# One hybrid RWKV-7 and RG-LRU step: the clock by which the scheduler orders the instructions is that of the timeline simulator

## Chip, cores and metric

The kernel runs on 1 core of one Trainium2 chip. The metric is the time of one execution in microseconds (us), the median of several runs. The engines are TensorE (PE in the rows; PEld is its weight load), VectorE (DVE), ScalarE (ACT), GpSimd (POOL) and SyncE (SP, which starts transfers).

## What is computed

One layer over 1152 tokens (128 of context, 1024 latent) of width 1024. An input projection feeds two token mixers side by side: RWKV-7 with 8 heads of 64 in two directions, and a bidirectional RG-LRU of 512 channels. Their outputs go through one output projection, and a gated feed-forward part with a convolution follows (inner width 2816).

```python
h = rmsnorm(x, lp['ln1_g']) * (1.0 + sc1) + sh1
proj = h @ lp['w_in']
r, k, v, xw, xa, xg, xb, gb = jnp.split(proj, SPLITS, axis=-1)
ya, s_fin = rwkv7_mix(r, k, v, xw, xa, xg, s0, ...)
yb, h_fin = rglru_mix(xb, gb, h0, ...)
x = x + g1 * (jnp.concatenate([ya, yb], axis=-1) @ lp['w_out'])
h = rmsnorm(x, lp['ln2_g']) * (1.0 + sc2) + sh2
u = dwconv(h @ lp['w_up'], ...)
ua, ub = jnp.split(u, 2, axis=-1)
x = x + g2 * ((jax.nn.gelu(ua) * ub) @ lp['w_down'])

def _wkv7_step(S, inp):          # per token, in both directions
    sa = jnp.einsum('dbhij,dbhj->dbhi', S, kk_t)
    S = S * w_t[..., None, :] - sa[..., :, None] * b_t[..., None, :] + v_t[..., :, None] * k_t[..., None, :]
    y = jnp.einsum('dbhij,dbhj->dbhi', S, r_t)
```

The bonus of RWKV-7 and the norms of its keys are sums over the 64 channels of a head; the kernel makes them on TensorE as small matmuls whose output has the tokens on the partitions (`cols2`).

## The kernel before

All products are in fp32, split into a high and a low part: one product is three matmuls, and the helper `mm` (L92) records all of them, so that the rows on TensorE have line 92 and are told apart by their tiles. A high part is rounded by L106 or L108, the low part is the remainder (L112).

The kernel is written as generators whose steps alternate at given rates (`beside`, `run_all`). That fixes the order in which the program is written. From it the language's scheduler makes one queue for each engine: it goes through the instructions with a simulated clock, takes among those that the clock says are ready the one written first, and so decides what stands behind what. On the chip each engine then works through its queue in that order and stops at an instruction whose input or buffer is not there. The stages, with the times of the profiled run:

- Start, 0 to 45 us: loads, first norm, transposes.
- A, 45 to 458 us: projections (tile mm; weights winp), one weight tile after the other, each in three spans of 384 tokens. Beside them run, as background generators, the preparation of the scan by `stage_ab`: rates and scaled keys on VectorE (L607 to L640), products dg, the bonus (kd on GpSimd, L669 and L670, then the head sums ab<-rkc,kd on TensorE and the copy bon at L503), the key norms (head sums uk, copy nsq at L503, key k at L572), and for each of four head pairs one `inverse` of 32x32 triangular blocks: a transpose (L510), 30 pairs of L517 and L519 on VectorE, transposes to T (L524) and TT (L526), then two rounds of matmuls iv with a ScalarE copy a2 (L539) between and the copy to TT (L553) behind, which is spilled to DRAM (L707). Values v are copied to vt (ScalarE, L825) and vr (VectorE, L826) and transposed on TensorE (pv, L832).
- B, 458 to 733 us: two scan lanes a and b. A lane goes through its 128-token tiles in hops of 64 tokens: G (mask, L1087, VectorE) from pa<-kxa,BK; Kt from transposes of BK (L1094); y from the state S and from G; R (L1077), V, the state's update (L1185, VectorE); outputs o (L1196, L1198). Beside them runs the rest of the projection with the RG-LRU: convolution taps (L853, VectorE), gates (matmuls lg, L898 on ScalarE), L909 to L919 with sqrt and exp on ScalarE, scans (L929).
- C, 733 to 967 us: four lanes a to d, the head norms of finished tiles (`post`, L1304 to L1322), the modulation vectors (md) and the RG-LRU half of the output projection (wo, gated in at L1408 and L1409).
- D, 967 to 1064 us: the RWKV half of the output projection and the second norm. E and F, from 1064 us on: up-projection (x, y, z, v) and down-projection (acc).

The lanes' buffers reuse the space of the inverse, so the lanes' first loads wait for the last spill of TT. The change touches the last lines of `kernel`; all that is told above lies in `tile_hybrid_step`, which it calls.

## Time and profile before

| | us |
|---|---|
| median of 3 runs (1865.54 to 1865.95) | 1865.56 |
| the profiled execution | 1856.04 |
| its span | 1854.3 |
| TensorE busy | 1699.7 |
| VectorE busy | 1271.6 |
| ScalarE busy | 852.6 |
| GpSimd busy | 727.1 |

The profiled execution is 9.5 us shorter than the median of the runs; 1.7 us of it lie outside the span. The mean granted clock of TensorE is 0.948 of full speed. The rows come from five views: the page; windows, which give the busy time of each engine in a stretch; waits, which sum an engine's idle time by the line that waited and what released it; the timeline, one engine's instructions in order with the idle time before each; and groups, which put alike instructions together.

### The profile page before, as it was taken

To read this page: it belongs to the slowest core of one execution; us is meant where nothing else is said; L and a number is where in the kernel's file an instruction comes from. 1 tells how busy PE (TensorE), PEld (TensorE's weight loads), DVE (VectorE), ACT (ScalarE), POOL (GpSimd) and SP (SyncE) were. 2 spreads that over 40 slices of the span, in tenths; PEclk is the share of its full clock that TensorE was granted. 3 is DMA by queue.
4 is the path that set the end of the run, shared out by engine and by line. 5 is a ranking of instruction groups with operands and counts; after the bars stand their busy time and mean duration, and the time that the engine had idled before them with its cause. 6 is when DMAs were issued, how large, how long until landed. Compare 5 with 4: busy or idle time off the path is not lost.

```text
span 1854.3 us, 35789 instructions
## 1 busy us (share of the span) xinstructions
PE 1699.7 (92%) x13365; PEld 1465.5 (79%) x13365; DVE 1271.6 (69%) x2635; ACT 852.6 (46%) x1763; POOL 727.1 (39%) x742
## 2 busy tenths in 40 slices
PE   5997889788999989799997789999999999999996
PEld 4786868588778778456665689999999999788885
DVE  6458797884467664467788867777777668576764
ACT  6456554642656666334324844444444443121211
POOL 1023332321254354131111076666666664434340
PEclk9998898898989999899998899999999999999998
DMA  8255454443433433856776222222222225548571
GB/s 299 63 163 155 163 162 148 149 128 120 128 107 97 134 103 112 267 192 228 232 245 209 103 65 84 72 72 73 82 73 72 74 81 169 187 161 262 179 247 57
DMA packets 268429, 264.94 MB, mean 143 GB/s; under 512 B 21173, under 2 KB 218448, under 8 KB 268256
## 3 DMA queue, kind: packets, MB, share of 16 engines
q1 hardware_dynamic: 252496, 245.97, 41.7%
q10 hardware_dynamic: 15472, 16.54, 2.6%
q8 instruction: 106, 1.74, 0.4%
q14 instruction: 67, 0.55, 0.1%
q0 software_dynamic: 288, 0.14, 0.0%
HBM read 188.00 MB, written 74.58 MB: 142 GB/s over the span
## 4 chain that ended last, share of the span: by engine, by line
PE 63%; DVE 7%; DMA 3%; issue 3%; ACT 3%; POOL 2%; SPq 0%; DVEq 0%; ACTq 0%; POOLq 0%
PE acc L92 14%; PE x L92 7%; PE y L92 7%; PE z L92 7%; PE mm L92 6%; PE v L92 3%; PE wo L92 3%; PE lg L92 2%; PE ya L92 2%; PE md L92 2%; PE pa L92 2%; PE yb L92 1%; PE ca L92 1%; PE pb L92 1%; PE cb L92 1%
## 5 line engine op out<-in xcount | busy, mean ns | idle before, releaser
L92 PE MATMUL mm<-h_hi,winp 128*128 128x384 f32 x1056 | 307.8, 363 | 6.9 <-DVE vr L826 5.9
L92 PEld LDWEIGHTS mm<-h_hi,winp 128*128 128x128 f32 x1056 | 204.2, 201 | 14.9 <-DVE vr L826 7.0
L92 PE MATMUL mm<-h_lo,winp 128*128 128x384 f32 x528 | 189.6, 360 | 3.7 <-DVE h_lo L112 3.7
L112 POOL TENSOR_TENSOR wl<-raw,wh 128x512 fp32r<-128x512 f32 x110 | 155.3, 1413 | 71.2 <-ACT wh L106 70.8
L106 ACT ACTIVATE wh<-raw 128x512 fp32r<-128x512 f32 x110 | 69.3, 632 | 149.0 <-PE z L92 81.0
L92 PE MATMUL x<-f_hi,wh 128*128 128x256 f32 (+1 forms) x352 | 105.9, 301 | 8.9 <-ACT q L1652 5.3
L92 PEld LDWEIGHTS mm<-h_lo,winp 128*128 128x128 f32 x528 | 106.4, 202 | 6.9 <-DVE h_lo L112 5.0
L1090 POOL TENSOR_TENSOR BK<-BK,pc 128x256 f32<-128x256 f32 x72 | 47.6, 663 | 157.2 <-PE pa L92 59.7
L92 PE MATMUL y<-t_hi,wh 128*128 128x320 f32 (+1 forms) x352 | 104.9, 298 | 0.9 <-DVE q L1657 0.9
L92 PE MATMUL x<-f_lo,wh 128*128 128x256 f32 (+1 forms) x352 | 105.5, 300 | 0.2 <-DVE f_lo L112 0.2
L92 PE MATMUL x<-f_hi,wl 128*128 128x256 f32 (+1 forms) x352 | 105.3, 299 | 0.0
L92 PE MATMUL y<-t_lo,wh 128*128 128x320 f32 (+1 forms) x352 | 104.7, 298 | 0.0
L92 PE MATMUL y<-t_hi,wl 128*128 128x320 f32 (+1 forms) x352 | 104.5, 297 | 0.0
L112 POOL TENSOR_TENSOR wl<-S,wh 128x512 fp32r<-128x512 f32 x44 | 57.5, 1308 | 105.7 <-ACT wh L106 105.7
L92 PE MATMUL acc<-f_hi 128*128 128x512 f32 x330 | 88.9, 390 | 2.7 <-ACT zf L1760 2.7
L108 POOL TENSOR_SCALAR t_hi<-raw 128x512 fp32r<-128x512 f32 x66 | 55.8, 846 | 76.0 <-PE acc L92 33.5
L1619 DVE SCALAR_TENSOR_TENSOR zf<-C,fcw,zf 128x567 f32<-128x567 f32 x66 | 63.0, 955 | 23.4 <-ACT zf L1617 23.4
L92 PEld LDWEIGHTS x<-f_hi,wh 128*128 128x128 f32 x352 | 67.9, 193 | 9.9 <-ACT q L1652 5.8
L92 PEld LDWEIGHTS acc<-f_hi 128*128 128x128 f32 x330 | 61.8, 188 | 15.9 <-ACT zf L1760 3.1
L112 DVE TENSOR_TENSOR t_hi<-raw,t_hi 128x512 fp32r<-128x512 f32 x66 | 47.0, 715 | 35.3 <-POOL t_hi L108 35.3
L1617 ACT ACTIVATE zf<-C,colB,fcw 128x576 f32<-128x576 f32 x66 | 57.2, 867 | 29.9 <-DVE C L1689 15.4
L92 PEld LDWEIGHTS x<-f_lo,wh 128*128 128x128 f32 x352 | 68.0, 193 | 0.5 <-DVE f_lo L112 0.4
(511 smaller groups left out, 5175.8 us busy)
## 6 DMA issues: line engine op xcount, KB each, us to landing
raw<-in_w_down SPq DMA_DIRECT2D x132, 256.0 KB, 3.1
raw<-in_w_up SPq DMA_DIRECT2D x88, 256.0 KB, 2.9
wmod<-in_w_mod SPq DMA_DIRECT2D x68, 256.0 KB, 4.6
act_d<-zf SPq DMA_DIRECT2D x44, 288.0 KB, 2.4
src<-act_d SPq DMA_DIRECT2D x66, 192.0 KB, 3.6
win<-in_w_in SPq DMA_DIRECT2D x44, 256.0 KB, 3.0
KR<-kb_d SPq DMA_DIRECT2D x36, 256.0 KB, 3.0
VS<-v_d SPq DMA_DIRECT2D x36, 256.0 KB, 3.5
```

The source lines that it names most:

```text
L92: PE.matmul(out, lhsT, rhs, start=start, stop=stop, skip_group_check=True)
L106: A.activation(hi, src, AF.Copy)
L108: eng.tensor_scalar(hi, src, 1.0, 0.0, op0=OP.mult, op1=OP.add)
L112: eng.tensor_tensor(lo, src, hi.bitcast(F32), op=OP.subtract)
L1090: G.tensor_tensor(bk, bk, pc_f[q.f][:, :, x:x + 1].to_broadcast([128, 2, 128]), op=OP.mult)
L1617: A.activation(u, src, AF.Identity, scale=fcw[:, 1, m:m + 1], bias=colb("ffn_conv_b", m))
L1619: V.scalar_tensor_tensor(dv[:, :, 1:64], sv[:, :, 0:63], fcw[:, 0, m:m + 1], dv[:, :, 1:64], op0=OP.mult, op1=OP.add)
```

## The change

The scheduler's simulated clock comes from the timeline simulator, where it came from the core simulator. What is written, the tiles, the pools and the rates stay.

```diff
@@ -1853,7 +1853,7 @@
-    with _tile.TileContext(nc) as tc:
+    with _tile.TileContext(nc, schedule_with_timeline_sim=True) as tc:
         tile_hybrid_step(tc, aps, *outs)
```

The instructions are the same, except for ScalarE's table loads: 29 before, 33 now. What differs is each engine's order, from the start to 1064 us; in the feed-forward part TensorE's order is as before but for one exchange of neighbours where E ends.

The first place is on TensorE in stage A, at a v projection. A group mm_3766 is copied to vt_3866, which pv_3946 transposes; mm_3961 and mm_4118 are the next two groups. Before:

```order
L92 MATMUL mm_3766<-h_hi_583,winp_3507 128x384
L92 MATMUL mm_3961<-h_hi_454,winp_3507 128x384
L92 MATMUL mm_3961<-h_lo_455,winp_3507 128x384
L92 MATMUL mm_3961<-h_hi_454,winp_3507 128x384 x2
L832 MATMUL pv_3946<-ident_96,vt_3866 128x128 x3
L92 MATMUL mm_3961<-h_lo_455,winp_3507 128x384
L92 MATMUL mm_3961<-h_hi_454,winp_3507 128x384
L92 MATMUL mm_3961<-h_hi_497,winp_3507 128x384
L92 MATMUL mm_3961<-h_lo_498,winp_3507 128x384
L832 MATMUL pv_3953<-ident_96,vr_3867 128x128 x3
```

and with the change (the rows left out are the rest of mm_3961 and most of mm_4118):

```order
L92 MATMUL mm_3766<-h_hi_583,winp_3507 128x384
L92 MATMUL mm_3961<-h_hi_454,winp_3507 128x384
...
L92 MATMUL mm_4118<-h_lo_541,winp_3507 128x384
L832 MATMUL pv_3946<-ident_96,vt_3866 128x128
L92 MATMUL iv_2932<-TT_2646,a2_2831 32x32 x32
L92 MATMUL ab_3872<-xa_s_90,lr_hi_3780 128x128
L92 MATMUL ab_3872<-xa_s_90,lr_lo_620 128x128
L92 MATMUL ab_3876<-xw_s_89,lr_hi_3780 128x128
L92 MATMUL ab_3876<-xw_s_89,lr_lo_620 128x128
L832 MATMUL pv_3946<-ident_96,vt_3866 128x128 x2
L92 MATMUL mm_4118<-h_hi_540,winp_3507 128x384
```

The transposes stood four matmuls behind the end of the group that they read; now they stand a whole group and most of the next behind it, and rounds of the inverse (iv) and of the rates (ab) stand between them.

The second place is on VectorE in the last of the four inverses, where gt and X are the inverse's own tiles, and xc, gw and winp belong to the RG-LRU and to the projection weights. The rows around the first two foreign instructions in it before:

```order
L517 TENSOR_TENSOR gt<-X 128x168
L519 TENSOR_TENSOR X<-X,gt 128x24x7
L112 TENSOR_TENSOR winp<-win,winp 128x512
L517 TENSOR_TENSOR gt<-X 128x184
L519 TENSOR_TENSOR X<-X,gt 128x23x8
L112 TENSOR_TENSOR winp<-win,winp 128x512
L517 TENSOR_TENSOR gt<-X 128x198
L519 TENSOR_TENSOR X<-X,gt 128x22x9
```

and the middle of it with the change:

```order
L112 TENSOR_TENSOR gwl<-gw,gwh 128x512
L519 TENSOR_TENSOR X<-X,gt 128x22x9
L853 SCALAR_TENSOR_TENSOR xc<-mm,colB,xc 128x126
L853 SCALAR_TENSOR_TENSOR xc<-mm,colB,xc 128x4x62
L517 TENSOR_TENSOR gt<-X 128x210
L853 SCALAR_TENSOR_TENSOR xc<-mm,colB,xc 128x127
L853 SCALAR_TENSOR_TENSOR xc<-mm,colB,xc 128x4x63
L519 TENSOR_TENSOR X<-X,gt 128x21x10
L853 SCALAR_TENSOR_TENSOR xc<-mm,colB,xc 128x127
L853 SCALAR_TENSOR_TENSOR xc<-mm,colB,xc 128x4x63
L517 TENSOR_TENSOR gt<-X 128x220
L519 TENSOR_TENSOR X<-X,gt 128x20x11
```

Before, 4 foreign instructions stand between its first and its last row, now 23: 12 of L853, 9 of L112 and 2 of L910.

The third place is on TensorE at the end of stage A, where pa<-kxa,BK is the first matmul of the scan, T_4844 and a_4974 belong to the last inverse, and lg are the RG-LRU's gates. Before:

```order
L92 MATMUL mm<-h_hi,winp 128x384
L92 MATMUL iv<-T_4844,off 32x32 x32
L92 MATMUL mm<-h_hi,winp 128x384
...
L92 MATMUL mm<-h_hi,winp 128x384
L92 MATMUL iv<-TT,a_4974 32x32 x32
L92 MATMUL mm<-h_hi,winp 128x384
L92 MATMUL mm<-h_lo,winp 128x384
...
L92 MATMUL mm<-h_lo,winp 128x384
L92 MATMUL pa<-kxa,BK 128x256 x2
L92 MATMUL mm<-h_hi,winp 128x384 x2
```

where the last iv row stands 36 rows (54 matmuls) ahead of pa; and with the change:

```order
L92 MATMUL mm<-h_lo,winp 128x384
L92 MATMUL mm<-h_hi,winp 128x384
L92 MATMUL lg<-xh,gwh 128x384
L92 MATMUL iv<-T_4844,off 32x32 x32
L92 MATMUL iv<-TT,a_4974 32x32 x32
L92 MATMUL lg<-xh,gwh 128x384
L92 MATMUL lg<-xl,gwh 128x384
L92 MATMUL lg<-xh,gwl 128x384
L92 MATMUL lg<-xl,gwh 128x384
L92 MATMUL lg<-xh,gwl 128x384
L92 MATMUL pa<-kxa,BK 128x256 x2
L92 MATMUL lg<-xh,gwh 128x384
```

Five gate matmuls stand now between the last matmul of the inverse and the first of the scan. Ahead of that first one, 72 more projection matmuls and 57 more gate matmuls stand than before. At the other end of the scan, the last matmul of wo stood one hop before the scan's end; with the change 167 rows of TensorE, those of the lanes and of the head norms, stand behind it.

## Rows read from the trace of the kernel before

**Rows 1.** The page: busy time of each engine, share of the span, instructions:
```profile
PE 1699.7 (92%) x13365; PEld 1465.5 (79%) x13365; DVE 1271.6 (69%) x2635; ACT 852.6 (46%) x1763; POOL 727.1 (39%) x742
```

**Rows 2.** Windows: stretch, length, busy us by engine, granted clock, DMA share, GB/s:
```profile
45.00:458.00 413.00, 353.60 (x3906) 315.99 (x3905) 297.86 (x606) 218.66 (x483) 111.20 (x150) 0.88 0.43 137
458.00:733.00 275.00, 262.54 (x2296) 212.62 (x2297) 169.78 (x341) 174.42 (x355) 120.86 (x124) 0.94 0.37 113
733.00:967.00 234.00, 219.47 (x1750) 144.68 (x1750) 151.55 (x440) 88.78 (x244) 47.79 (x72) 0.96 0.72 233
967.00:1064.00 97.00, 74.41 (x351) 56.87 (x348) 85.58 (x214) 62.53 (x147) 9.52 (x10) 0.87 0.50 165
1064.00:1555.00 491.00, 484.83 (x3613) 484.10 (x3613) 346.41 (x580) 219.69 (x351) 323.35 (x244) 0.99 0.24 76
```

**Rows 3.** Windows of two stretches inside stage A:
```profile
160.00:270.00 110.00, 94.77 (x1238) 83.71 (x1236) 97.99 (x213) 65.03 (x155) 38.27 (x52) 0.91 0.46 144
310.00:431.00 121.00, 100.49 (x1134) 89.92 (x1132) 107.27 (x250) 56.63 (x126) 30.07 (x38) 0.90 0.42 132
```

**Rows 4.** VectorE waits in stage A: line, releaser, us in total, times, longest:
```profile
DVE bon L503 <- PE ab L92: 15.5, 8, 4.7
DVE nsq L503 <- PE uk L92: 15.3, 9, 3.7
DVE k L572 <- PE uk L571: 6.1, 5, 3.0
```

**Rows 5.** What TensorE waited for in stage A, same columns:
```profile
PE ab L92 <- POOL kd L670: 13.8, 5, 4.7
PE pv L832 <- ACT vt L825: 4.7, 3, 3.4
```

**Rows 6.** Windows of 10 us in stage A:
```profile
350.00:360.00 10.00, 2.70 (x28) 1.76 (x28) 9.07 (x24) 5.43 (x12) 2.68 (x4) 0.65 0.58 197
360.00:370.00 10.00, 8.06 (x86) 6.59 (x87) 8.69 (x16) 5.49 (x15) 3.19 (x5) 0.50 0.60 177
```

**Rows 7.** Timeline, VectorE, last inverse: start, us, engine, line, operation, tiles:
```profile
401.74 2.00 DVE L510 STREAM_TRANSPOSE X<-ds 128x1024 f32<-128x1024 f32 x1
...
409.31 0.69 DVE L112 TENSOR_TENSOR winp<-win,winp 128x512 fp32r<-128x512 f32 x1
...
430.93 1.92 DVE L526 STREAM_TRANSPOSE TT<-X 128x1024 f32<-128x1024 f32 x1
```

**Rows 8.** Timeline, TensorE, end of stage A; in brackets idle before, releaser:
```profile
446.66 0.44 PE L92 MATMUL mm<-h_hi,winp 128*128 128x384 f32 x1
...
455.79 0.34 PE L92 MATMUL mm<-h_lo,winp 128*128 128x384 f32 x1
...
458.25 1.54 PE L92 MATMUL pa<-kxa,BK 128*128 128x256 f32 x4 [2.13 <-ACT xc L875]
```

**Rows 9.** Windows at the end of stage C:
```profile
920.00:940.00 20.00, 20.00 (x177) 13.85 (x176) 17.18 (x54) 6.42 (x20) 3.44 (x5) 1.00 0.69 218
```

**Rows 10.** Groups of VectorE, whole run: busy us, mean ns, idle before:
```profile
L853 DVE SCALAR_TENSOR_TENSOR xc<-mm,colB,xc 128x378 f32<-128x378 f32 x16 | 9.6, 600 | 0.2
L910 DVE SCALAR_TENSOR_TENSOR th<-th,xc 128x1152 f32<-128x1152 f32 x8 | 11.4, 1426 | 5.1 <-ACT th L898 5.1
L1087 DVE TENSOR_TENSOR G<-pa,mask 128x512 f32<-128x512 f32 x32 | 22.0, 689 | 18.1 <-PE pa L92 17.8
L1185 DVE TENSOR_TENSOR S1a<-ca,S1a 64x128 f32<-64x128 f32 x32 | 9.2, 287 | 7.1 <-PE ca L92 6.7
L1308 DVE TENSOR_TENSOR v<-v,bon 128x256 f32<-128x256 f32 x16 | 7.1, 444 | 0.1
```

**Rows 11.** Timeline of TensorE, two pieces of a scan hop in stage B:
```profile
487.38 1.13 PE L92 MATMUL pa<-kxa,BK 128*128 128x256 f32 x4
...
488.44 0.45 PE L92 MATMUL cb<-VS,Kt 128*64 128x64 f32 x8
```

**Rows 12.** Groups of ScalarE, 45 to 450 us:
```profile
L128 ACT ACT_TABLE_LOAD x4 | 5.1, 1283 | 0.1
```


## The prediction

> **What bounds the kernel now.** I read the page's busy times first. TensorE is busy for 92% of the span and VectorE for 69% [rows 1], but these are means over stages with different limits, so the windows by stage come next [rows 2]. The reader is to see two things in them. From 1064 us on (the feed-forward part) TensorE is full, 484.8 of 491 us, and the listing of the two orders shows its queue there as before but for one exchange of neighbours, so that part gets 0. In stage A, 45 to 458 us, TensorE is busy for 353.6 of 413 us, so it idles for 59 us, at a granted clock of 0.88. Stages B and C have it at 262.5 of 275 and 219.5 of 234 us: there TensorE is the limit, and work taken out of them saves its own time. Stage D, 967 to 1064 us, has VectorE at 85.6 of 97 us.
>
> The third view splits stage A. From 160 to 270 us VectorE is busy for 98.0 of 110 us, from 310 to 431 us for 107.3 of 121 us [rows 3]. So stage A is a chain on VectorE with TensorE's gaps around it. The waits say what the chain waits for where it does wait: the copies of the head sums bon, nsq and the normalised key k wait 15.5, 15.3 and 6.1 us for TensorE [rows 4], 36.9 us together, because TensorE's queue held projection matmuls ahead of the small ones. In the other direction TensorE waits 13.8 us for GpSimd's kd and 4.7 us for ScalarE's vt [rows 5]: small matmuls that stand in the queue before their input is there. What such a wait costs beyond itself stands in two windows: TensorE is busy for 2.7 us of 350 to 360 us, and in the next 10 us its clock is 0.50, the lower of its two levels (1.2 GHz instead of 2.4) [rows 6].
>
> **The change part by part.** The change touches no instruction but 4 more ScalarE table loads; it gives every engine's queue another order up to 1064 us. I cost the places at which the order differs most. The profiled run took 1856.0 us (span 1854.3) and the median of the runs is 1865.6, 9.5 more; the sum is made on the profiled run, and I add the same 9.5.
>
> *Stage A, small matmuls behind their producers.* In the changed order a v transpose stands 5 to 10 us of matmuls behind the end of the group it reads, where it stood mostly 0.7 (four matmuls), and the first six of twelve bonus matmuls stand 7 to 12 us of work later. TensorE's waits of rows 5 lose their cause there. For VectorE it can go either way: its copies also stand later in its own queue, so other work fills the time. Of its 36.9 us of waits between none and all go; nothing in the trace of before settles where between, so I take half: **-18**.
>
> *Stage A, the last inverse.* VectorE's last inverse runs without a break from 401.7 to 432.9 us [rows 7], and its end releases everything that the scan needs. Before, 4 foreign instructions stand in it (the row at 409.3, 0.69 us each, 2.8 us). In the changed order there are 23: 12 of L853 at about 0.5 (the widest takes 0.600), 9 of L112 at 0.69 and 2 of L910 at 1.43 [rows 7, 10], 15.1 us. That is **+12** on the path to the first scan matmul, less if some of them run where the inverse would wait; it has no such wait now, so I take all of it.
>
> *The border of A and B.* Before, TensorE runs 54 projection matmuls from 446.7 to 455.8 us after the last inverse matmul, and then waits 2.1 us for the first scan matmul at 458.25 us [rows 8]. That is 11.6 us from the last inverse matmul, a chain of a copy, a spill and two loads that the order cannot shorten. In the changed order five gate matmuls stand there, at the 0.17 us spacing of rows 8 (9.1 us for 53 steps) 0.9 us. So TensorE will idle some 10.7 us there, and some 3.4 more because the two copies between the inverse's matmul pairs lose their cover too: 14 where there were 2.1. What is late next is unchanged, the first scan matmul: the chain from VectorE's last transpose to it comes out at 25 to 27 us in both orders. It is priced by where the covering work went: 72 projection and 57 gate matmuls now stand ahead of the first scan matmul, 129 x 0.17 = 22 us. So the first scan matmul goes from 458 to 458 - 18 + 12 = 452 us, **-6**, and 22 us less work is left for B and C.
>
> As a check, TensorE's idle time in stage A becomes 59 - 6 - 22 = 31 us, 14 of it at the border, so 17 for the rest against 57. This is a lot to ask, and it is the weakest link.
>
> *Stages B and C.* TensorE bounds them [rows 2], so the 22 us of work that have gone ahead are worth **-22** while it stays the bound.
>
> *The end of stage C.* There it does not stay the bound. Before, matmuls of the LRU half of the output projection (wo) fill TensorE's gaps until the last hop of the scan. In the changed order they are used up early, and 167 rows of scan and head-norm matmuls follow alone, some 20 hops. Their pieces run from 0.45 to 1.13 us [rows 11], about 4 us for the six of a hop, so 80 us for all if none overlaps the next, some 65 if each gives 0.1 to 0.15 to it; I take 72. VectorE has in the same stretch 17 masks (L1087, 0.689 us), 74 state and output additions (0.287), 9 head norms at ten operations of about 0.43 and some small ones (4.8), and 6 weight remainders of the shape of the row at 409.3, 0.69: 11.7 + 21.2 + 43.2 + 4.1 = 80 us [rows 7, 10]. So VectorE is the bound there, and every hop hands over to it and back. With VectorE full that is 80 us, 8 more than TensorE's 72; at the share of the stretch at 920 to 940 us, 17.2 of 20 [rows 9], it is 93, 21 more; at the mean of stage C, 151.6 of 234 [rows 2], 124, 52 more. I take **+15**, between the first two, since the stretch at 920 us is the one with the same mix of work.
>
> *Stage D.* Six of the weight remainders that VectorE makes in stage D now stand ahead of the end of the scan, 6 x 0.69 = **-4**, VectorE being the limit there [rows 2].
>
> *ScalarE.* The LRU quarters in stage B now need four table loads each instead of two, 18 in the stage for 12 and 33 in all for 29, at 1283 ns [rows 12]: 7.7 us more in a stage where ScalarE is busy for 174 of 275 us [rows 2], so 0. The Trainium skill, "ScalarE: Activation LUTs", "Rules for kernel authors", says to group transcendentals by table set, which this order breaks; its section "What ACT_TABLE_LOAD costs" gives about 2.66 us for a switch, load and drain. The trace's row agrees with the load of 1283 ns; by the page six more switches would be 16 us of ScalarE, by the row 7.7.
>
> The sum: -6 - 22 + 15 - 4 = -17, so 1839 for the profiled run and **1848** for the median (1865.6 less 17, rounded down).
>
> **The rivals.** *VectorE becomes the bound at the end of the scan, and the time is lost there.* For it: it loses its cover of wo matmuls, and each hop needs five or so hand-overs to VectorE that queue behind head-norm operations. Against it: at 920 us VectorE runs at 86% with the same mix. Its price lies between +21 and +52; with the middle, +37, and with stage A saving none of its waits (+12), it is 12 - 22 + 37 - 4 = +23, so 1889. It decides from +32 in that tail if stage A gives its 6, from +14 if A loses 12.
>
> *The gaps of stage A all close and the clock comes back.* If only the 14 us at the border stay, 45 of 59 us of idle time go, the 6 and the 22 among them. A clock of 0.88 is 24% of 413 us at the lower level, 99 us; less the 59 idle, at least 40 us of work ran at half speed and lost 20 us. Then it is -45 - 20 + 15 - 4 = -54, so 1812. For it: the low clock stands behind the gaps [rows 6]. Against it: 14 us of idle time at one place are new, and VectorE still limits the stage. The Trainium skill's page "TensorE: Matmul & The Clock Gate", section "HAM oscillation — how this bites in real kernels", describes the same loss, bursts of matmuls that run slow behind idle gaps; the clock of 0.50 behind the gap at 350 us agrees.
>
> *ScalarE delays the scan's copies.* If the 7.7 us of further loads fall on copies that a hop waits for, the sum is -9, 1856.
>
> *All is given back*: a tail of +32 with the 6 of stage A leaves 0, 1862 to 1869. That the change does nothing at all is excluded by the orders, which differ in every stage up to 1064 us.
>
> **How the numbers follow.** The forecast has 0.42, closed gaps with the clock 0.13, ScalarE 0.05, all given back 0.08, the slower tail 0.32. A measurement of this kernel can tell about 0.2%, 3.7 us, from no change. The first three are faster by more than that, 0.60; the fourth is the same, 0.08; the last slower, 0.32. The range goes from 1812, which leaves out about half of the second case, to 1890, which leaves out the dearer part of the tail's bounds, some 0.18 in all. The forecast's own range is 1835 to 1861, by half the VectorE waits either way (18) cut to what the check on TensorE's idle time allows.
>
> **What would show it.** In the profile of the changed kernel: the first scan matmul near 452 us (470 if stage A saves nothing), behind a TensorE gap of about 10 us; the waits of bon, nsq and k on VectorE near 18 us in sum; TensorE's clock in stage A above 0.88; the last wo matmul some 80 to 95 us before the end of the scan, and VectorE above 85% from there on with TensorE below full; second norm and up-projection following 4 us sooner after the scan's end; the feed-forward part as long as before. I am wrong if TensorE's idle time in stage A is not below 45 us, if the tail takes over 105 us, or if the feed-forward part changes by more than 2 us.

## The result and the profile after

The changed kernel takes **1878.93 us** (median of 6 runs, 1872.82 to 1882.66) where the kernel before takes 1863.64 in the same comparison (6 runs, 1855.92 to 1865.95). The ratio is 1.009, with a 95% interval of 1.0066 to 1.0115: slower by 0.9%, some 15 us. The time lies inside the range that was given, but on the other side of no change.

Both kernels spread over some 10 us between runs, and the profiled run of before, 1856.0, lies 7.6 us below the median of its six; that of after, 1878.3, lies at its own. So the two profiles differ by 22.1 us of span where the medians differ by 15, and a few us between two profiles decide nothing. What the stages are worth is taken from ratios of medians further down; the profiles say where to look.

The page of the changed kernel, its first rows (as [rows 1]):

```profile
span 1876.4 us, 35922 instructions
PE 1701.6 (91%) x13365; PEld 1480.4 (79%) x13365; DVE 1291.0 (69%) x2635; ACT 850.9 (45%) x1767; POOL 723.4 (39%) x742
```

Seen over the whole span nothing has happened: TensorE is busy for 1701.6 us instead of 1699.7. Next come windows between events that both kernels have: start of the last inverse (402 us in both), first scan matmul (458.2 before, 481.0 after), first matmul of the up-projection (1041 and 1065; it runs ahead of the last matmuls of the output projection, so before 1064 us, where stage D was said to end), end. Columns as in [rows 2]; busy time of TensorE is the third number, the granted clock the third from the end. First the kernel before:

```profile
45.00:402.00 357.00, 303.12 (x3369) 267.77 (x3369) 265.63 (x528) 203.03 (x456) 99.97 (x131) 0.88 0.45 142
402.00:458.20 56.20, 50.47 (x539) 48.21 (x537) 32.42 (x79) 15.64 (x28) 11.23 (x20) 0.88 0.33 104
458.20:1041.00 582.80, 542.13 (x4318) 402.32 (x4319) 387.26 (x950) 305.53 (x698) 178.09 (x205) 0.94 0.54 172
1041.00:1854.00 813.00, 779.08 (x4950) 728.71 (x4948) 557.81 (x956) 299.97 (x526) 431.39 (x370) 0.98 0.36 116
```

and the changed kernel:

```profile
45.00:402.00 357.00, 314.19 (x3502) 290.23 (x3495) 264.51 (x524) 199.47 (x459) 92.44 (x126) 0.91 0.46 147
402.00:481.00 79.00, 51.85 (x511) 46.66 (x510) 57.38 (x113) 38.74 (x52) 28.95 (x31) 0.79 0.22 68
481.00:1065.00 584.00, 530.08 (x4192) 393.64 (x4193) 361.89 (x908) 286.03 (x670) 158.79 (x194) 0.93 0.53 169
1065.00:1876.00 811.00, 778.52 (x4949) 728.98 (x4947) 574.37 (x960) 296.70 (x529) 434.74 (x370) 0.98 0.37 116
```

Five readings. Up to 402 us TensorE idles less, 42.8 us (357.00 - 314.19) instead of 53.9, and gets 133 more matmuls done. From there to the first scan matmul it idles 27.2 us instead of 5.7. From the first scan matmul to the up-projection it has 126 matmuls less to do and needs 584 us for them instead of 582.8: idle time rises from 40.7 to 53.9 us, and the matmuls that are left are no cheaper. The feed-forward part is 1.7 us shorter in its span. And from 45 us to the up-projection as a whole TensorE is busy for 895.7 us before and 896.1 us with the change (the first three rows of each table added up), while its idle time rises from 100.3 to 123.9 us: the time by which the profile of the change is longer is time in which TensorE waits.

In the inverse on VectorE, the answer to [rows 7] (timeline of VectorE in the changed kernel; in brackets the idle time before and who ended it):

```profile
402.36 2.10 DVE L510 STREAM_TRANSPOSE X<-ds 128x1024 f32<-128x1024 f32 x1
...
414.98 0.69 DVE L112 TENSOR_TENSOR gwl<-gw,gwh 128x512 fp32r<-128x512 f32 x1 [2.72 <-POOL gwh L108]
...
426.20 0.60 DVE L853 SCALAR_TENSOR_TENSOR xc<-mm,colB,xc 128x372 f32<-128x372 f32 x1 [2.46 <-ACT xc L875]
...
449.43 2.00 DVE L526 STREAM_TRANSPOSE TT<-X 128x1024 f32<-128x1024 f32 x1
```

It takes 49.1 us (402.36 to 451.43) instead of 31.1. The two rows in the middle are foreign instructions that not only take their own time but stand there and wait for GpSimd and ScalarE, with the inverse's steps queued behind them.

The border on TensorE, the answer to [rows 8] (timeline of TensorE in the changed kernel):

```profile
463.37 1.20 PE L92 MATMUL iv<-T,off 32*32 32x32 f32 x64
...
469.12 1.92 PE L92 MATMUL iv<-TT,a 32*32 32x32 f32 x64 [4.55 <-ACT a L539]
...
473.62 0.69 PE L92 MATMUL lg<-xh,gwh 128*128 128x384 f32 x1 [2.58 <-DVE xc L853]
...
477.88 0.69 PE L92 MATMUL lg<-xl,gwh 128*128 128x384 f32 x1 [3.56 <-DVE xl L112]
...
481.07 2.05 PE L92 MATMUL pa<-kxa,BK 128*128 128x256 f32 x4 [1.55 <-DMA BK<-kb_d]
```

The projection matmuls of [rows 8] are gone from here. In the brackets stand the gaps that they covered: 4.55 us for the ScalarE copy between the inverse's two rounds, and 2.58 and 3.56 us in which even the few gate matmuls that stand here wait for VectorE.

### The profile page after: what moved, and what is told of

It reads as the page before. It is cut to its first block, busy times and chain, and to the rows that moved or that the text cites. A ratio compares the mean times of both kernels' runs of the same rounds, so it can differ in the third digit from the quotient of the medians.

```text
span 1876.4 us, 35922 instructions
## 1 busy us (share of the span) xinstructions
PE 1701.6 (91%) x13365; PEld 1480.4 (79%) x13365; DVE 1291.0 (69%) x2635; ACT 850.9 (45%) x1767; POOL 723.4 (39%) x742
## 4 chain that ended last, share of the span: by engine, by line
PE 62%; DVE 13%; ACT 6%; DMA 5%; issue 4%; POOL 2%; SPq 0%; DVEq 0%; ACTq 0%; POOLq 0%
PE acc L92 14%; PE x L92 7%; PE z L92 7%; PE y L92 7%; PE mm L92 7%; PE v L92 3%; PE wo L92 3%; PE md L92 2%; PE lg L92 2%; PE ya L92 2%; DVE X L519 2%; PE pa L92 2%; DVE gt L517 1%; PE yb L92 1%; PE pb L92 1%
## 5 line engine op out<-in xcount | busy, mean ns | idle before, releaser
L112 POOL TENSOR_TENSOR wl<-raw,wh 128x512 fp32r<-128x512 f32 x110 | 148.6, 1352 | 132.6 <-ACT wh L106 132.5
L92 PE MATMUL y<-t_hi,wh 128*128 128x256 f32 (+1 forms) x352 | 104.6, 297 | 0.0
L92 PE MATMUL y<-t_lo,wh 128*128 128x256 f32 (+1 forms) x352 | 104.5, 297 | 0.0
L92 PE MATMUL y<-t_hi,wl 128*128 128x256 f32 (+1 forms) x352 | 104.2, 296 | 0.0
L112 POOL TENSOR_TENSOR wl<-S,wh 128x512 fp32r<-128x512 f32 x44 | 57.5, 1308 | 116.3 <-ACT wh L106 116.3
L112 DVE TENSOR_TENSOR t_hi<-raw,t_hi 128x512 fp32r<-128x512 f32 x66 | 49.4, 754 | 37.1 <-POOL t_hi L108 37.1
L92 PEld LDWEIGHTS acc<-f_hi 128*128 128x128 f32 x330 | 61.9, 188 | 12.8
L92 PEld LDWEIGHTS x<-f_hi,wl 128*128 128x128 f32 x352 | 68.2, 194 | 0.0
```

What stands on the lines that cost most here:

```text
L92: PE.matmul(out, lhsT, rhs, start=start, stop=stop, skip_group_check=True)
L112: eng.tensor_tensor(lo, src, hi.bitcast(F32), op=OP.subtract)
```

## The experiments

All kernels below compute what the kernel before computes; they differ in the order of the queues, and where a sentence says so in where the program writes a step. Ratios are of medians to the kernel before, run beside them. The changed kernel's is 1.0090 [1.0066, 1.0115].

**1. The long inverse.** If the first scan matmul sets the time, work of stage B must not stand in the inverse. VectorE's part of it is queued behind the inverse's last transpose:

```diff
-    run_all((take(lane_a, LA), LA), (take(lane_b, LB), LB), (rest_of_projection(), ...))
+    with tc.issue_after(inv_end[0]): run_all((take(lane_a, LA), LA), (take(lane_b, LB), LB), (rest_of_projection(), ...))
```

> The changed kernel, with one edit: on VectorE everything of stage B (the RG-LRU work that had moved into the last inverse, and the scan) is queued behind the last transpose (L526) of the last inverse. Theory A (the loss is made in the last inverse, where 23 foreign instructions cost VectorE 18 us, and in the copies behind it): the last inverse takes 31 to 33 us instead of 49, the first scan matmul moves from 481 to about 460 us, and the time falls by 15 to 20, to 1859 to 1864 us. Theory B (the loss is made at the end of the scan, where the output-projection matmuls are missing; what is gained at the first scan matmul is given back there): the first scan matmul also moves, but the time stays within 4 us of 1879.

Measured: 1.0086 [1.0055, 1.0117], 1878.44 us. The first scan matmul moved from 481.1 to 452.5 us, 28.6 us forward, to where the prediction had wanted it, and the time stayed. Windows of this kernel, from 402 us to its first scan matmul and from there to its up-projection:

```profile
402.00:452.50 50.50, 23.85 (x380) 21.28 (x375) 33.06 (x80) 12.76 (x22) 10.82 (x18) 0.67 0.25 78
452.50:1061.40 608.90, 556.89 (x4290) 413.11 (x4291) 382.98 (x936) 306.06 (x693) 175.56 (x203) 0.93 0.52 164
```

and TensorE's largest wait from 45 to 452 us (total, times, longest):

```profile
PE iv L92 <- DVE T L524: 19.3, 3, 17.6
```

TensorE's idle time up to the scan is the changed kernel's (26.7 us for 27.2), 17.6 us of it in one wait for the transposed inverse. What went is work: 23.9 us of matmuls stand between 402 us and the first scan matmul where 51.9 stood, because the gate and projection steps need VectorE steps that the edit moved back. They run behind that matmul, 98 matmuls more in 608.9 us instead of 584. The first scan matmul is not the measure.

**2. The end of the scan without wo.** Each group of wo matmuls is bound behind the scan hop that the program writes before it, by an order of issue without a wait, so that the scheduler cannot use them up early:

```diff
-                    mix_mm(ps, k, ys, wo, cs)
+                    pin(mix_mm(ps, k, ys, wo, cs))
```

> The changed kernel, with one edit: each matmul group of the LRU half of the output projection (wo) is queued on TensorE behind the scan hop that was written before it, so that these matmuls are spread to the end of the scan as in the kernel before. Theory A: stage A is unchanged (first scan matmul at 481 us); the stretch of 101 us between the last wo and the last hop is worth what TensorE idles there, at most 29 us, and the time falls by 5 to 15, to 1864 to 1874. Theory B: the tail is the whole loss, and the time falls by 20 to 29, to 1850 to 1859. A third: TensorE is not what the scan waits for there, and nothing changes, 1879 within 4.

Measured: 1.0078 [1.0044, 1.0113], 1876.91 us. Windows of this kernel: the end of the scan, up to the first matmul of the output projection's RWKV half (mm<-woh), and from there to the up-projection:

```profile
888.00:984.00 96.00, 88.86 (x712) 61.20 (x711) 69.01 (x192) 31.18 (x92) 16.58 (x23) 1.00 0.49 155
984.00:1064.20 80.20, 63.60 (x254) 47.53 (x255) 63.58 (x154) 39.01 (x93) 8.50 (x8) 0.83 0.53 175
```

The window of the changed kernel from its last wo matmul to its last state addition:

```profile
888.00:989.20 101.20, 82.60 (x791) 60.63 (x790) 76.89 (x234) 40.33 (x123) 26.23 (x38) 0.86 0.34 101
```

The edit did what it was for: the clock is 1.00 instead of 0.86 there, the scan ends 18 us sooner (970.7 instead of 989.2), TensorE idles 7 us instead of 18.6. But the output projection then takes 80.2 us where it takes 67.8 in the changed kernel, and the time stays.

**3. Both edits.**

> The changed kernel with both edits: stage B behind the last inverse on VectorE, and the wo matmuls behind their scan hops on TensorE. Theory A (both losses are separate): the sum of the two, 1844 to 1859 us, below the kernel before. Theory B (the second edit alone does it): as the second edit alone, within 4 us.

Measured: 1.0073 [1.0045, 1.0100], 1876.47 us. Two stretches that look like the loss are mended, and some 14 us (0.73% of 1860.75) stay lost. So mending these places does not bring the time back.

**4. The other way round: the inverse filled under the old order.** With the scheduler of before, the program writes the first RG-LRU steps ahead of the last inverse:

```diff
+    while bg_i.step():
+        for _ in range(1):
+            if n_ahead < 20:
+                next(rest)
```

> The kernel before with the core simulator's order, with one edit: the first steps of the RG-LRU are written ahead of the last inverse, so that TensorE's queue has 72 more projection matmuls and 54 more gate matmuls ahead of the first scan matmul (as the changed order has), while VectorE's last inverse holds the same 4 foreign instructions as before. Theory A (work pulled ahead is worth its time as long as TensorE bounds stages B and C): first scan matmul within 8 us of 458, the time 10 to 22 us lower than before, 1842 to 1854. Theory B (what is pulled ahead is missing as cover later): the time within 4 us of before, 1864.

Measured: 1.0051 [1.0026, 1.0076], 1871.1 us. The first scan matmul comes at 506.4 us, 48 later than before, for 9.5 us of time. TensorE's waits from 433 to 507 us:

```profile
PE lg L92 <- DVE xc L855: 10.0, 2, 5.5
PE lg L92 <- DVE xl L112: 9.7, 1, 9.7
```

Gate matmuls in front of the first scan matmul wait 19.7 us for their inputs, and most of it is given back: from the first scan matmul to the up-projection takes 546.8 us instead of 582.9. Again that matmul moves far and the time does not follow. Neither theory had this time: the pulled work gained nothing, and 9.5 us were lost besides.

**5 and 6. One stage's order at a time.** The program is built twice, with either scheduler. In the second build each engine's queue is bound, instruction by instruction and by order of issue alone, to that of the first up to the first scan instruction of that engine; the rest is left to the second build's scheduler:

```diff
+    for a, b in zip(head, head[1:]):
+        tc.add_manual_dep(b, a.name, dep, reason="order of the other scheduler")
...
+    order = _queues(build(None, True)[1])
+    nc, tc, arrays = build(order, False)
```

(True is the timeline simulator's clock. These lines are of kernel 6; kernel 5 has the two swapped.) Kernel 5 has stage A in the order of before and the rest ordered by the timeline clock:

> All engines keep the order of the kernel before up to the first instruction of the scan; from there on the order is the timeline simulator's. What the runs so far show is that TensorE's busy time up to the up-projection is the same in all of them (917 to 923 us), so that the time goes with TensorE's idle time alone: 120 us before and 142 us with the change, of which stage A has 10 more (with 12 us of work pulled into it) and the scan and stage D 13 more. Theory C (the two halves are separate losses): the first scan matmul at 458 us, the up-projection starts 11 to 15 us later than before, the time is 1872 to 1877. Theory D (the loss is in stage A alone and what follows only repeats it): as before, 1861 within 4. Theory E (the loss is in the scan's half alone): 1880 within 4.

Measured: 1.0183 [1.0142, 1.0223], 1896.05 us, slower than any of its three theories. Kernel 6 has stage A in the changed order and the rest in the order of the core simulator's clock:

> The reverse: all engines keep the changed order up to the first instruction of the scan, and from there on the order is the core simulator's. Theory C: the first scan matmul at 481 us, stages B to D as good as before with 12 us of their matmuls already done, so 10 us above before, 1868 to 1873. Theory D: as the changed kernel, 1879 within 4. Theory E: as before, 1861 within 4.

Measured: **0.9955 [0.9932, 0.9977]**, 1851.75 us, faster than both kernels, which no theory gave either. Its windows, cut at the same events (the first scan matmul at 489.2, the up-projection at 1035 us):

```profile
45.00:402.00 357.00, 315.87 (x3428) 292.10 (x3427) 261.54 (x523) 199.91 (x458) 93.72 (x126) 0.90 0.46 147
402.00:489.20 87.20, 57.65 (x589) 51.57 (x589) 60.07 (x115) 42.26 (x58) 28.78 (x32) 0.78 0.23 72
489.20:1035.00 545.80, 508.29 (x4177) 371.15 (x4178) 358.38 (x910) 277.96 (x661) 157.74 (x193) 0.96 0.57 179
```

The first two rows look like the changed kernel's, long inverse and idle border included. The third is 38.2 us shorter than the changed kernel's (545.8 for 584.0) with 15 matmuls less: 16.4 us less idle time (37.5 for 53.9), and 21.8 us less busy time, of which 15 matmuls at the stretch's own mean (508.29 by 4177, 0.12 us) make up 2. So the changed order of stage A is worth some 8.4 us (0.45% of 1863.6), and the changed order of the rest costs more than that.

The second half of this reading needs the rest of kernel 6 to stand in the order of before, since the scheduler makes the rest anew behind the bound part. The traces allow a count: of the instructions from the first scan matmul to the up-projection, the share that the longest common order of two queues takes in. Kernel 6 and the kernel before share 91 to 93% on each of TensorE, VectorE, ScalarE and GpSimd, where before and the change share 44 to 65%. Kernel 5 shares only 61 to 69% with the changed kernel: behind the old stage A the timeline clock made a third order, so kernel 5 does not show what the changed order of the rest costs. Other edits move more than they name too: kernels 1, 3 and 7 share 58 to 79% with the change and kernels 12 and 13 only 56 to 67%, while kernel 2 stays near it (79 to 95%).

**7 and 8. ScalarE's table loads.** In the changed kernel each square root of a quarter is put behind the quarter's last exponential, which leaves 27 loads in all for 33; kernel 8 does the same in kernel 5:

```diff
-            A.activation(a2, a2, AF.Sqrt, scale=0.25)
+            sq = A.activation(a2, a2, AF.Sqrt, scale=0.25); tc.add_manual_dep(sq.ins, ex.ins.name, ..., reason="sqrt last")
```

> The changed kernel, with one edit: in each quarter of the RG-LRU the square roots are queued on ScalarE behind the last exponential of the quarter, so that ScalarE loads 27 tables instead of 33, 12 instead of 18 in stage B. Theory F (in stage B the scan's copies on ScalarE wait behind table loads, 9.7 us of TensorE's waits at rows of VS, R, Kt and o of ScalarE against 0.8 before): TensorE's waits on ScalarE between 481 and 700 us fall below 4 us and the time falls by 5 to 8, to 1871 to 1874. Rival: the loads lie where nothing waits, and the time stays within 3 of 1879.

> Order of before up to the scan, the timeline simulator's from there on, and the square roots behind the last exponential of their quarter (29 table loads, as before, instead of 35). Against the same without that edit: theory F 5 to 8 us less, the rival within 3.

Measured: 1.0151 [1.0115, 1.0187], 1885.1 us, and 1.0184 [1.0158, 1.0209], 1893.49 us (kernel 5: 1.0183). Fewer loads gain nothing in either place. In the changed kernel the time even rises, with intervals that just meet; whether by the later square roots or by what else the scheduler moved is not shown. No gain came from loading less.

**9 to 11. Where the order is changed back.** As kernel 6, with the bound part ending at the third and fourth lane's first instruction (start of stage C), at the output projection (start of D), and, shorter than in kernel 6, at the start of the last inverse:

```diff
-    run_all((lane_a, 98 - LA), (lane_b, 98 - LB), (lane_c, 26), (lane_d, 26), (posts(90), 90),
+    run_all((lane_a, 98 - LA), (lane_b, 98 - LB), (watch(lane_c), 26), (watch(lane_d), 26), (posts(90), 90),
```

> The changed order in stages A and B (up to the first instruction of the lanes c and d on each engine), the core simulator's from there on. With the changed order in stage A alone the time was 1852, in all stages 1879, so 27 us are lost between the first scan matmul and the up-projection. Theory G (they are lost in stage B, where the lane copies of VectorE and ScalarE stand behind work of the RG-LRU): 1872 to 1880. Theory H (they are lost in stage C and its end, where the wo matmuls are used up 100 us early and TensorE's clock falls to 0.81 to 0.86): 1850 to 1856. In between, the excess over 1852 is stage B's share.

> The changed order in stages A to C, the core simulator's for what is written behind the scan (second norm and feed-forward part). If stage D's own order matters (10.5 us of idle TensorE there against 7.8), 1872 to 1876; if it only takes over what stage C leaves, 1879 within 3.

> The changed order up to the start of the last inverse at 402 us, the core simulator's from there on. Up to there the changed order has 11 us less idle TensorE than before (43 for 54), and from there to the first scan matmul 22 more. If the gain of stage A lies ahead of the last inverse and the rest of the stage spoils it, the core simulator's own order behind the cut gives 1846 to 1850; if the pulled work only runs out at the last inverse whatever the order there is, 1852 within 3, as with the changed order in the whole of stage A.

Measured, as ratios to before in the order of how much has the changed order:

| changed order up to | ratio | interval | median |
|---|---|---|---|
| start of the last inverse (kernel 11) | 0.9942 | 0.9916 to 0.9968 | 1849.4 |
| first scan instruction (kernel 6) | 0.9955 | 0.9932 to 0.9977 | 1851.75 |
| start of C (kernel 9) | 1.0048 | 1.0026 to 1.0071 | 1870.81 |
| start of D (kernel 10) | 1.0131 | 1.0092 to 1.0169 | 1885.35 |
| up-projection (the change) | 1.0090 | 1.0066 to 1.0115 | 1878.93 |

All the gain is in by the start of the last inverse. Between the first scan instruction and the start of C the ratio rises by 0.0093, some 17 us, and the two intervals are apart. From C on it rises by another 0.0042, 8 us, to the change itself, with intervals that just overlap. Kernel 10, slower than either value expected of it, lies above both; that C alone costs 15 and D gives 8 back is what the medians say, but the intervals of kernel 10 and of the change overlap, so this split stays open.

**12 and 13. Work ahead of the scan.** In kernel 6 the scan hops come sooner: lane a's fifteenth hop starts at 601 us, in the changed kernel at 677, before at 607. Theory: the changed order lets gate and projection matmuls go ahead of the hops, the hops slip, and the end of the scan stands alone. So, with stage A bound to the changed order and the rest made by the timeline clock, these matmuls are bound behind the hops that the program writes ahead of them; kernel 13 binds wo as well:

```diff
-            mm3(ps[:, 0:b - a], (w[0][:, k, :], w[1][:, k, :]), hilo(k, slice(a, b)), k == 0, k == 7)
+            pin2(mm3(ps[:, 0:b - a], (w[0][:, k, :], w[1][:, k, :]), hilo(k, slice(a, b)), k == 0, k == 7))
```

> The changed order in stage A, the timeline simulator's order from there on, with one edit: in stage B each TensorE group of the RG-LRU and of the projection (lg, mm) that does not stand in the queue ahead of the first scan matmul is queued behind the scan hop written before it. With the changed order in A and B, lane a is at its hop 15 (of 32) at 674 us and at hop 20 at 748 us, with the core simulator's at 601 and 649 us, though its first hop is at the same time: filling matmuls stand ahead of the scan. Theory J (this alone makes stage B's share, 17 us of the 27): hop 15 near 610 us and 1858 to 1866 us for the time. Rival (the order of VectorE and ScalarE in stage B costs by itself): the hops come earlier, but the time stays at 1875 or above.

> The same, and in stage C the wo groups too are queued behind the scan hop written before them. Theory J: 1850 to 1860, most of the way to the 1852 of the kernel that has the core simulator's order from the first scan matmul on. Rival: as with the wo groups held in the changed kernel (1877), no gain beyond that of the first edit.

Measured: 1.0142 [1.0117, 1.0167], 1891.17 us, and 1.0133 [1.0107, 1.0158], 1888.6 us. In kernel 12 the fifteenth hop starts at 619 us instead of 677, and the time gets worse. The window of kernel 12 from its first scan matmul to the up-projection:

```profile
478.90:1077.80 598.90, 534.62 (x4192) 395.45 (x4193) 363.40 (x908) 284.63 (x668) 155.52 (x194) 0.93 0.52 164
```

Its two largest waits of TensorE from 481 to 740 us (total, times, longest):

```profile
PE pa L92 <- ACT Kt L1096: 4.8, 2, 3.7
PE ca L92 <- DVE VS L1078: 4.7, 3, 3.1
```

The early hops wait for their copies (Kt, VS) on ScalarE and VectorE, with TensorE's other work held behind them. Earlier hops by themselves do not bring the time, so the theory is not borne out; what the rest of these kernels' new order does to the time is not told apart from it.

**14 and 15. Which engine's queue.** The order of stage A stays the changed one in both. From the scan on, kernel 14 gives TensorE alone kernel 6's order and lets the timeline clock order the others around it; kernel 15 gives VectorE, ScalarE and GpSimd that order and lets the timeline clock order TensorE around them:

```diff
+    order2 = _queues(build(order, False)[1])
+    ENG[:] = ['PE']
+    nc, tc, arrays = build(order2, True)
```

(kernel 15 has `['DVE', 'Activation', 'Pool']`.)

> The changed order in stage A; from the first scan matmul on, TensorE alone has the order that the core simulator gives (as in the kernel of 1852 us), and the other engines are ordered by the timeline simulator around it. Theory K (TensorE's own order in stages B and C makes the loss: too little other work between a scan matmul and the copy that the next one reads): 1850 to 1858, and TensorE's waits for scan copies of ScalarE and VectorE back to about 12 us from 32. Theory L (the order on VectorE and ScalarE makes it): 1872 or above.

> The reverse: from the first scan matmul on, VectorE, ScalarE and GpSimd have the core simulator's order, and TensorE's is the timeline simulator's. Theory K: 1870 or above. Theory L: 1850 to 1860. If both this and the other stay near 1852, or both rise, the orders only fit together and neither engine's alone is the cause.

Measured: 1.0102 [1.0069, 1.0134], 1880.14 us, and 1.0273 [1.0239, 1.0307], 1913.71 us. Neither comes near kernel 6's 0.9955, so no one of these queues brings the time along. That the loss lies in no single queue does not follow, because the queues left free are not the changed kernel's. In kernel 14 VectorE, ScalarE and GpSimd share 49, 55 and 68% of their order with the change, hardly more than those of before do (44, 52 and 65%); in kernel 15 TensorE shares 56% (before: 51%). And SyncE's queue, which starts the transfers, has the faster schedule's order in neither: TensorE's largest wait in kernel 14 is for a transfer of modulation weights. The window of kernel 14 from its first scan matmul to the up-projection, and that wait:

```profile
487.59:1069.20 581.61, 516.31 (x4179) 374.37 (x4180) 363.71 (x915) 285.14 (x672) 151.41 (x193) 0.95 0.53 168
PE md L92 <- DMA wmod<-in_w_mod: 9.6, 2, 5.5
```

**What the scan waits for.** TensorE's waits that are named by their releaser, line by line: before and in kernel 6 there are few, in the changed kernel many. The three largest of before, 458 to 733 us:

```profile
PE ca L92 <- DVE R L1077: 4.9, 1, 4.9
PE ya L92 <- DVE S0a L1185: 2.5, 1, 2.5
PE pa L92 <- ACT xc L875: 2.1, 1, 2.1
```

The three largest of kernel 6, 489.2 to 740 us:

```profile
PE ca L92 <- DVE R L1077: 4.9, 1, 4.9
PE lg L92 <- ACT gt L789: 2.1, 2, 1.2
PE ca L92 <- DVE VS L1077: 1.9, 1, 1.9
```

And of the changed kernel, over the longer stretch of 481 to 888 us:

```profile
PE pa L92 <- DMA BK<-kb_d: 4.2, 3, 2.1
PE ya L92 <- ACT VS L1075: 2.5, 2, 2.2
PE ca L92 <- ACT R L1075: 2.5, 1, 2.5
PE yb L92 <- DVE S1b L1185: 2.5, 2, 2.3
```

Summed over all such groups from the first scan matmul to the up-projection, pieces of scan hops wait for a copy of VectorE or ScalarE 15 times before (19.1 us), 11 times in kernel 6 (12.2 us), 41 times in the changed kernel (32.5 us), 42 times in kernel 5 (39.7 us) and 39 times in kernel 12 (33.6 us). From before to the change that is 13.4 us more, as much as TensorE's idle time there grows (40.7 to 53.9 us). The mean granted clock of the stretch is 0.94 before, 0.96 in kernel 6, 0.93 in the changed kernel and kernel 12, 0.91 in kernel 5. In these five, more small waits and a lower clock go together, and much the same matmuls take longer at the lower clock (4177 in 508.3 us at 0.96, 4192 in 530.1 us at 0.93). Neither is a measure of the loss by itself. The same sums give 12 waits and some 14 us for kernel 11, the fastest, at a clock of 0.94, and 29 waits and some 22 us at 0.95 for kernel 14, which is as slow as the change: its TensorE idles 65.3 us, mostly at other places. The Trainium skill, "TensorE: Matmul & The Clock Gate", section "HAM oscillation — how this bites in real kernels", describes bursts of matmuls that run slow behind long waits for transfers. The trace agrees only in that more idle time and a lower clock stand in one stretch: the waits listed here are short and mostly for copies.

## Why the prediction went wrong, step by step

**The sum again.** Cut at the first scan matmul and at the first matmul of the up-projection, the windows give each part of the sum as measured. In stage A TensorE's idle time was to fall by 28 us (59 to 31) and rose by 10 (59.6 to 70.0). The work pulled ahead was to be 22 us; 12 more us of busy time stand ahead of the scan and 12 less behind it. From the scan to the up-projection idle time was to rise by 11 us (+15 and -4) and rose by 13. So the step that failed in the sum is the idle time of stage A, 38 us off: 29 of them are the date of the first scan matmul (the -18 came out as nothing, the +12 as 18, the chain behind the inverse as 4 longer), the rest is the pulled work, 10 us smaller than forecast. The experiments add a second one, that the pulled work would be worth its time in B and C: that holds under one order and not under the other.

**Less waiting of VectorE in stage A, -18: the step that failed.** The waits of [rows 4] did what was forecast and more: bon, nsq and k wait 14.4 us (1.5, 10.2, 2.7) instead of 36.9. But VectorE did not run further for it. Its waits in the changed kernel from 45 to 402 us, the largest and those of [rows 4]:

```profile
DVE winp L112 <- ACT winp L106: 20.7, 7, 7.4
DVE b L617 <- DMA rk<-kk_d: 11.3, 5, 4.9
DVE nsq L503 <- PE uk L92: 10.2, 4, 4.0
DVE gt L517 <- PE iv L92: 9.7, 2, 6.0
...
DVE k L572 <- PE uk L571: 2.7, 4, 1.2
...
DVE bon L503 <- PE ab L92: 1.5, 1, 1.5
```

Other instructions wait in their place: weight remainders (winp, 12.8 us before), rates behind a load (b), the next inverse's steps (gt). VectorE idles 92.5 us from 45 to 402 us where it idled 91.4, and the last inverse starts at 402.36 where it started at 401.74. The prediction asked how many of the waits go, and never what is late next, for a wait on an engine that works through its queue in order. The gain of stage A came from the other engine: TensorE's idle time to 402 us fell by 11.1 us, and its clock rose from 0.88 to 0.91.

**The last inverse, +12:** 18. The foreign work was about right: VectorE's busy time inside the inverse goes from 27.8 to 38.6 us, +10.8. The other 7.2 us are its idle time there, 3.3 to 10.5. "Less if some of them run where the inverse would wait" looked only in one direction: an instruction brought in from elsewhere brings its own producer's delay with it.

**The border and the first scan matmul, 452 us:** it came at 481. The chain from the inverse's end to it takes 29.6 us instead of 25.4, forecast 25 to 27; TensorE idles 27.2 us from 402 us to it instead of 5.7. The check that the prediction put to itself, idle time of stage A from 59 to 31 us, came out at 70 (42.8 and 27.2), which is past the 45 that it named as the point of being wrong. But the 29 us between 452 and 481 are not the loss either: kernel 1 takes nearly all of them away and gains nothing, and kernel 6, with as much idle time in stage A as the change (70.7 us), has that matmul at 489 us and is the fastest but one. Up to there the matmul's own date was used as a measure of how far the kernel has got. It is one only where the same work lies ahead of it. By ratios the whole changed order of stage A is worth 8.4 us, where -6 and -22 had been put down for it.

**Stages B and C, -22 because TensorE bounds them: wrong.** A share of 95% [rows 2] under one order was taken as a property of the stage. It is one of the order: with 126 matmuls less to do, the changed kernel takes 1.2 us more for the stretch (584.0 for 582.8). Under the order of before the term comes out, and more: kernel 6, with 141 matmuls less than before, takes 37 us less for it (545.8). The order of B alone costs 17 us (kernel 6 to kernel 9). Of the rivals only one had the scan losing time before its end, ScalarE's table loads, at 7.7 us and a chance of 0.05.

**The end of stage C, +15: right in kind, and near in size.** The last wo matmul comes at 887.9 us, 101 us ahead of the last state addition (80 to 95 forecast, 105 named as too much); TensorE idles 18.6 us there at a clock of 0.86. VectorE, though, is busy for 76.9 of 101.2 us, 76% and not the 85% that would make it the bound: each engine waits for the other. C and D together cost 8 us by the table (kernel 9 to the change). Yet kernel 2 fills the stretch and the time stays, so this is a place where lost time shows, and not one that could be mended by itself. The slower rival, VectorE as the bound at the end of the scan, had the right sign for another reason: it put the loss at the end of the scan, and the table puts most of it ahead of C. The measured time lies inside the stated range only because this rival had stretched it upwards.

**Stage D, -4:** not resolved. In the profiles it is 12 us shorter counted from the last state addition (87.7 to 75.7) and 4.9 longer counted from the first matmul of the output projection (62.9 to 67.8), because the wo matmuls that ran in between before are done earlier now. The medians' -8 has an interval as wide as itself.

**ScalarE, 0: not contradicted**: 6 loads less gained nothing in kernels 7 and 8. The rule of the Trainium skill, "ScalarE: Activation LUTs", "Rules for kernel authors", is to group by table set; here doing so left the time at 1.0151 in place of 1.0090 and at 1.0184 in place of 1.0183, so no gain from it is measured.

**The feed-forward part, 0: right**, 1.7 us shorter in its span.

**What stays open.** The place is shown: the changed order gains 8 to 11 us by the start of the scan, loses 17 between the first scan instruction and stage C, and some 8 behind that. Which property of the scan's order does it is not. Fillers ahead of the hops (kernels 12, 13), wo (2, 3), square roots (7), TensorE's queue (14) and the other engines' (15) were each put back without getting the time back, but mostly with the other queues made anew around them, so none of them is excluded as a part of it; SyncE's queue was never put back by itself. The count of waits for copies accounts for the idle time that the change adds behind stage A, and no kernel changed that count alone.

**A better version.** Kernels 6 and 11, with the changed order up to the last inverse (kernel 11) or up to the scan (kernel 6) and the old one from there, take 0.9955 [0.9932, 0.9977] and 0.9942 [0.9916, 0.9968] of the time before; they cannot be told apart.

## What to carry to other kernels

A new order of the queues is judged by TensorE's busy time plus its idle time up to an event that has the same work ahead of it in both kernels, and not by the date of the first step of the next stage: here that date moved by 29 us forward without a trace in the time, and by 48 back for 10 us of it. An edit under a scheduler moves more than it names, so compare the whole queues of two kernels before one cause is read from their times. A wait that vanishes from an in-order queue is a gain only once the next late instruction is named, and a stage's share of busy time holds for the order it was measured under. When a scheduler's clock is exchanged, try it stage by stage: the two halves of this change had opposite signs, and binding the first stage to one order and leaving the rest to the other was faster than either.

## What the runs showed that was not expected

- The same matmuls do not take the same busy time under another order: from the first scan matmul to the up-projection, 4177 matmuls took 508.3 us at a mean granted clock of 0.96 (kernel 6), 4192 took 530.1 us at 0.93 (the change) and 534.6 us at 0.93 (kernel 12). No single gap was long: the largest wait in the changed kernel's list above is 2.5 us.
- The order of a faster kernel on some engines does not bring its time along: with kernel 6's order on TensorE and the others ordered around it by the timeline clock the ratio is 1.0102, with kernel 6's order on VectorE, ScalarE and GpSimd it is 1.0273, where kernel 6 itself has 0.9955.
- Six table loads of 1283 ns less on ScalarE, at 45% busy, came with no gain (1.0151 [1.0115, 1.0187] for 1.0090 [1.0066, 1.0115]; 1.0184 for 1.0183).
